# Between two layers of a transformer trunk: inverse roots, modulation and low parts change engines, and small matmuls change order

## The chip, the cores and the metric

One core of a Trainium2 chip runs the whole program. The engines are TensorE (PE in the profile, its weight loads PEld), VectorE (DVE), ScalarE (ACT), GpSimd (POOL) and SyncE (SP, which issues most DMAs). Each works through its own queue in order and waits there for semaphores of the others. The metric is device microseconds of one launch, the median of several runs.

## The reference

The trunk has two layers and a shared key/value step between them. D is 1024, the sequence 1024 tokens.

```python
h = _modulated_norm(x, norm_g[0], shift, scale)
y = _gdn_mixer(h, ...)                  # layer A: gated delta rule, 8 heads of 128
x = x + gate * y
hk = _modulated_norm(x, kv_norm_g, mkv[:, :D], mkv[:, D:])
kv = hk @ w_kv
k_sh = _rms(kv[..., :1024].reshape(B, T, 16, 64), k_gain); v_sh = kv[..., 1024:]
h = _modulated_norm(x, norm_g[1], shift, scale)
x = x + gate * _sb_mixer(h, k_sh, v_sh, ...)   # layer B: stick-breaking attention

# _modulated_norm: x * rsqrt(mean(x*x) + EPS) * gain * (1 + scale) + shift
```

Everything is in 32-bit floats. In layer A a unit lower triangular system of each chunk of 64 tokens is solved (`triangular_solve`).

## The kernel before

Tokens come in 8 tiles of 128. To keep 32-bit accuracy the kernel splits a matmul operand into a high part in the fast format `F32R` and a low part, the rest. `mm3` (L100 to L102) issues three matmuls for each product: high by high, high by low, low by high. So whoever makes an operand makes a high part (a cast) and then a low part (a subtraction that reads the cast).

Layer A runs up to about 700 us, a loop over 8 heads. In it `stage_d` (L549) inverts the triangular blocks of all 8 chunk pairs of a head: matmuls of 32x32 blocks into `py` (L560), copies `y1` on ACT, matmuls into `pu` (L567, L570), then the same with 64x64 blocks. The rows of a 32x32 matmul count two passes each, so 16 matmuls show as x32.

Behind it comes the stage that this text calls the bridge, about 711 to 787 us. `rest_of_a(t)` (L715) has two calls for each of the 8 tiles. The first call is the output projection of the last two heads: `split_o` brings `of` and makes `oh` (ACT, L226) and `ol` (DVE, L227), 12 matmuls of 512 columns fill `pj`, and L237 (DVE) adds the residual and gives `x2`. POOL issues its store (L727). ACT squares `x2` with a running sum (L729), DVE forms the inverse root (`rsqrt`, L86: a start value from integer operations and three Newton steps, 11 instructions on a 128x1 column, names `rsb_y` and `rsb_z`), and L732 scales `x2` in place. That write has to wait until the store of `x2` has landed (semaphores DMASW in the order's rows). The second call transposes the tile in two groups of four 128x128 blocks into the PSUM tile `ptx`, copies a group to `xh` (L740), stores `xh` for layer B, modulates its four blocks into `htk` (L744, a scale and a shift for each partition), casts the high part into `hkT` (L746, ACT) and subtracts for the low part (L747, POOL). `keys_values` then multiplies `hkT` with the key/value weights: `kv_half` (L775), matmuls of 256 columns; its norm of keys (`rnb`, 128x16) uses `rsqrt` too.

Only PE's order is written out by hand there:

```python
with tc.manual_schedule(engines={PE.engine}):
    ra, kv = [rest_of_a(t) for t in range(NT)], keys_values()
    for step in "01203w142k53k64k75kk6k7k":
        next(kv if step in "wk" else ra[int(step)], None)
```

A digit is a call for that tile (its first occurrence the projection, its second the transposes), `w` brings the first weights, `k` is one quarter of a `kv_half`, 24 matmuls. So tile 4 is projected after the transposes of tile 1, and so on. The order of the other engines' queues is made by the scheduler. `xh`, `htk` and two temporaries of `kv_half` share five buffers (tag `x2k`); `pj` has two PSUM buffers.

Of the kernel before, what the change touches and what calls it, by code (L numbers as in the profile page):

```python
# [8 lines left out]
F32 = mybir.dt.float32  # L9
F32R = mybir.dt.float32r  # L10
I32 = mybir.dt.int32
AF = mybir.ActivationFunctionType
ALU = mybir.AluOpType
# [9 lines left out]
def kernel(  # L23
# [24 lines left out]
    V, S, G, PE = nc.vector, nc.scalar, nc.gpsimd, nc.tensor  # L48
    dma = nc.sync.dma_start

    P = 128
# [5 lines left out]
    NC = T // P  # L57
# [28 lines left out]
    def rsqrt(pool, v, n, tag):  # L86

        y = pool.tile([P, n], F32, name=f"{tag}_y", tag=f"{tag}_y")
        z = pool.tile([P, n], F32, name=f"{tag}_z", tag=f"{tag}_z")
        yi = y.bitcast(I32)  # L90
        V.tensor_scalar(out=yi, in0=v.bitcast(I32), scalar1=1, scalar2=None, op0=ALU.arith_shift_right)
        V.tensor_scalar(out=yi, in0=yi, scalar1=-1, scalar2=0x5F3759DF, op0=ALU.mult, op1=ALU.add)
        for _ in range(3):
            V.tensor_tensor(out=z, in0=y, in1=y, op=ALU.mult)
            V.scalar_tensor_tensor(out=z, in0=z, scalar=-0.5, in1=v, op0=ALU.mult, op1=ALU.mult)
            V.scalar_tensor_tensor(out=y, in0=z, scalar=1.5, in1=y, op0=ALU.add, op1=ALU.mult)  # L96
        return y

    def mm3(ps, lh, ll, rh, rl, start, stop):
# [22 lines left out]
    mod_sh = [const.tile([P, ND], F32, name=f"sh{i}") for i in range(3)]  # L122
    mod_gs = [const.tile([P, ND], F32, name=f"gs{i}") for i in range(3)]
# [128 lines left out]
    with tc.tile_pool(name="st", bufs=2, side="right", reuse_waits="tile") as st:  # L252
# [54 lines left out]
        for n0 in (0, 512):  # L307
            scale = mod_acc(st, 0, 1, n0, 512, 16)
# [7 lines left out]
            for hf in range(TH):  # L316
# [13 lines left out]
                  start=True, stop=True)  # L330
# [11 lines left out]
    with tc.tile_pool(name="gt", bufs=1, side="right", reuse_waits="tile") as gt:  # L342
# [6 lines left out]
        for cc in range(NC):  # L349
# [6 lines left out]
        y = gt.tile([P, HA, NC], F32, name="gy")  # L356
        V.tensor_tensor(out=y, in0=pbv[:, 8:16, :], in1=alb[:, 1, :][:, :, None].broadcast_to([P, HA, NC]),
                        op=ALU.add)
# [11 lines left out]
        for cf in coef[2:]:  # L370
# [10 lines left out]
                               op0=ALU.mult, op1=ALU.mult)  # L381
# [4 lines left out]
        f = lambda a: a.rearrange("p h c -> p (h c)")  # L386
# [32 lines left out]
    for i in range(2):  # L419
        U = gp.tile([P, NC, P], F32, name=f"U{i}")  # L420
# [128 lines left out]
    def stage_d(h, st):  # L549
        U, nm = st["U"], st["nm"]  # L550

        for b in range(3):
            bs = slice(32 * b, 32 * b + 32)
            c0 = 32 * (b % 2)
            V.transpose(out=tb[bs, :, c0:c0 + 32], in_=U[bs, :, bs])
        blk = [slice(32 * b, 32 * b + 32) for b in range(4)]
        py = dd_pool.tile([P, NC, 32], F32, name="py", tag="dd")
        for a in (0, 2):
            for cc in range(NC):
                PE.matmul(py[blk[a + 1], cc], nm[blk[a], cc, blk[a + 1]], tb[blk[a], cc, 0:32],  # L560
                          start=True, stop=True)
        y1 = gp.tile([P, NC, 32], F32, name="y1", tag="y1")
        for a in (0, 2):
            S.copy(out=y1[blk[a + 1]], in_=py[blk[a + 1]])
        pu = dd_pool.tile([P, NC, 32], F32, name="pu", tag="dd")
        for cc in range(NC):
            PE.matmul(pu[blk[1], cc], U[blk[1], cc, blk[1]], y1[blk[1], cc], start=True, stop=True)  # L567
        for a in (0, 2):
            for cc in range(NC):
                PE.matmul(pu[blk[a], cc], y1[blk[a + 1], cc], U[blk[a + 1], cc, blk[a + 1]],  # L570
                          start=True, stop=True)
        S.mul(out=tb[blk[1], :, 0:32], in_=pu[blk[1]], mul=-1.0)
        for a in (0, 2):
            S.mul(out=U[blk[a], :, blk[a + 1]], in_=pu[blk[a]], mul=-1.0)
        lo_, up_ = slice(0, 64), slice(64, 128)
        py = dd_pool.tile([P, NC, 64], F32, name="py2", tag="dd")
        for cc in range(NC):
            PE.matmul(py[up_, cc], nm[lo_, cc, up_], tb[lo_, cc], start=True, stop=True)
        y2 = gp.tile([P, NC, 64], F32, name="y2", tag="y2")
        S.copy(out=y2[up_], in_=py[up_])  # L580
        pu = dd_pool.tile([P, NC, 64], F32, name="pu2", tag="dd")
        for cc in range(NC):
            PE.matmul(pu[lo_, cc], y2[up_, cc], U[up_, cc, up_], start=True, stop=True)
        S.mul(out=U[lo_, :, up_], in_=pu[lo_], mul=-1.0)
# [62 lines left out]
    for h in range(HA):  # L647
# [23 lines left out]
        if h < len(mods):  # L671
            i, part = mods[h]
# [33 lines left out]
    hkT = xsp.tile([P, 2, ND, T], F32R, name="hkT")  # L706

    kp_ = kv_stack.enter_context(tc.tile_pool(name="kvp", bufs=2, side="right", reuse_waits="tile"))
# [6 lines left out]
    def rest_of_a(t):  # L715
        x2 = None
        if t in early:
            xr, o, x2 = early[t]
        else:
            o = split_o(kp_, oTa, t, rest, "of", 2, kp_, ("oh", "ol"))  # L720
            xr = x4([P, D], F32, "xr")
            dma(out=xr, in_=xs1[t])
        x2 = x2 or x4([P, D], F32, "x2")
        for hf in range(2):
            sl = slice(hf * 512, hf * 512 + 512)
            out_proj(o, wo, rest, hf, xr[:, sl], x2[:, sl])
        G.dma_start(out=xs2[t], in_=x2)  # L727
        sv = kp_.tile([P, 1], F32, name="sv", tag="sv")
        S.activation(out=xr, in_=x2, func=AF.Square, accum_out=sv)  # L729
        V.tensor_scalar(out=sv, in0=sv, scalar1=1.0 / D, scalar2=EPS, op0=ALU.mult, op1=ALU.add)  # L730
        rs = rsqrt(kp_, sv, 1, "rsb")
        V.tensor_scalar(out=x2, in0=x2, scalar1=rs, scalar2=None, op0=ALU.mult)  # L732
        yield
        ts_ = slice(t * P, (t + 1) * P)
        for kk in range(0, ND, 4):
            pt = wk_pool.tile([P, 4, P], F32, name="ptx", tag="wk")
            for i in range(4):
                PE.transpose(pt[:, i], x2[:, (kk + i) * P:(kk + i + 1) * P], ident)
            xh = kp_.tile([P, 4, P], F32, name="xh", tag="x2k", bufs=5)
            S.copy(out=xh, in_=pt)  # L740
            dma(out=xhT[kk:kk + 4, :, ts_].rearrange("k p t -> p k t"), in_=xh)
            ht = kp_.tile([P, 4, P], F32, name="htk", tag="x2k", bufs=5)
            for i in range(4):
                V.tensor_scalar(out=ht[:, i], in0=xh[:, i], scalar1=mod_gs[2][:, kk + i:kk + i + 1],  # L744
                                scalar2=mod_sh[2][:, kk + i:kk + i + 1], op0=ALU.mult, op1=ALU.add)
            S.copy(out=hkT[:, 0, kk:kk + 4, ts_], in_=ht)  # L746
            G.tensor_tensor(out=hkT[:, 1, kk:kk + 4, ts_], in0=ht, in1=hkT[:, 0, kk:kk + 4, ts_],  # L747
                            op=ALU.subtract)


# [24 lines left out]
    def kv_half(n, parts, hf):  # L775
        c0 = n * 256
        kv = x4([P, 4, 256], F32, "kv")
        n2 = kp_.tile([P, 4, 4], F32, name="n2b", tag="n2b") if n < 4 else None
# [20 lines left out]
            return  # L799
        n2 = n2.rearrange("p t g -> p (t g)")  # L800
        V.tensor_scalar(out=n2, in0=n2, scalar1=1.0 / HD, scalar2=EPS, op0=ALU.mult, op1=ALU.add)
        rn = rsqrt(kp_, n2, 16, "rnb")
        kg = kv.rearrange("p t (g d) -> p (t g) d", d=HD)
        V.tensor_tensor(out=kg, in0=kg, in1=rn[:, :, None].broadcast_to([P, 16, HD]), op=ALU.mult)
        V.tensor_tensor(out=kg, in0=kg, in1=gain[:, 2:3, :].broadcast_to([P, 16, HD]), op=ALU.mult)
# [111 lines left out]
    n2, sqs, vraw = {}, {}, {}  # L917
# [258 lines left out]
```

## Time and profile before

| what | before |
|---|---|
| median of 3 runs | 1514.25 us (1512.17 to 1517.61) |
| the profiled execution | 1510.67 us, span 1508.8 us |
| granted TensorE clock, whole span | 0.983 |
| busy in the span: PE / DVE / ACT / POOL | 1408.9 / 1074.4 / 728.0 / 151.3 us |
| bridge, 711 to 787 us: PE / DVE / ACT / POOL | 56.77 / 71.89 / 40.43 / 26.52 us of 76.00 |

A row of a table by windows has, in this order, the stretch and its length, then the busy time of PE, PEld, DVE, ACT and POOL with their counts of instructions, the granted TensorE clock as a share of full speed, the busy share of the DMA engines and what they moved. A row of the timeline has the start, the duration, engine, line and operation, the tile written and the tiles read, and in brackets the idle time ahead of it and what ended it.

### The profile page before, as it was taken

The numbers are of one execution on the slowest core, as the hardware profiler recorded it, in microseconds if no ns is written. First come the engines' busy times: TensorE is split into PE (matmuls) and PEld (weight loads), VectorE is DVE, ScalarE is ACT, GpSimd is POOL, SyncE is SP. The second block draws the span as 40 slices with busy tenths as digits, with TensorE's granted clock in tenths as the row PEclk, the third lists the DMA queues.
The fourth block names the chain that finished last, engine by engine and source line by source line (L and its number), as shares of the span: only waits on it lengthen the run. The fifth ranks groups of instructions, "written<-read, shape, count | busy, mean of one in ns | idle before, by whom it ended". The sixth has DMA issues, their size and how long they took to land.

```text
span 1508.8 us, 23724 instructions
## 1 busy us (share of the span) xinstructions
PE 1408.9 (93%) x8739; PEld 1179.8 (78%) x8739; DVE 1074.4 (71%) x2595; ACT 728.0 (48%) x1429; POOL 151.3 (10%) x121
## 2 busy tenths in 40 slices
PE   3789999999979999999689999999999999998998
PEld 1478888787868887887589999888888888885676
DVE  3768796977868697855997710478888888889332
ACT  5456645545545554422554422366566666665210
POOL 1300000000000000000330111412121121100000
PEclk9999999999989999999899999999999999999999
DMA  9144324444443444445744343624224223324511
GB/s 331 50 126 137 74 49 117 115 137 114 122 106 116 104 147 119 146 124 171 264 154 155 140 141 105 182 57 112 78 64 112 82 83 88 95 74 132 170 54 57
DMA packets 175303, 181.18 MB, mean 120 GB/s; under 512 B 36617, under 2 KB 129618, under 8 KB 175186
## 3 DMA queue, kind: packets, MB, share of 16 engines
q1 hardware_dynamic: 174034, 175.46, 39.1%
q0 software_dynamic: 1152, 4.19, 0.7%
q8 instruction: 69, 1.13, 0.3%
q14 instruction: 48, 0.39, 0.1%
HBM read 140.22 MB, written 39.40 MB: 119 GB/s over the span
## 4 chain that ended last, share of the span: by engine, by line
PE 61%; DVE 26%; ACT 5%; DMA 4%; issue 2%; SPq 1%; POOL 0%; DVEq 0%; ACTq 0%
PE pj L100 14%; PE pj L102 14%; PE pj L101 14%; DVE kp L977 7%; DMA mraw<-in_w_ada_dram 2%; DVE wl L998 2%; PE ptw L991 2%; PE pgr L473 2%; DVE macc L139 2%; PE pa L1016 1%; ACT whi L183 1%; PE pa L1017 1%; DVE htk L744 1%; PE pl L968 1%; DVE qk L412 1%
## 5 line engine op out<-in xcount | busy, mean ns | idle before, releaser
L100 PE MATMUL pj<-hT,whi 128*128 128x512 f32 (+1 forms) x528 | 216.2, 410 | 6.0 <-ACT vT L410 3.1
L102 PE MATMUL pj<-hT,wlo 128*128 128x512 f32 (+1 forms) x528 | 215.8, 410 | 4.5 <-DVE wlo L184 4.4
L101 PE MATMUL pj<-hT,whi 128*128 128x512 f32 (+1 forms) x528 | 215.1, 407 | 1.2 <-POOL hT L298 1.2
L977 DVE TENSOR_TENSOR_SCAN kp<-kp 128x896 f32<-128x896 f32 (+7 forms) x128 | 190.4, 1490 | 12.1 <-ACT kp L973 10.8
L973 ACT ACTIVATE kp<-pl,nrq 128x512 f32<-128x512 f32 (+1 forms) x192 | 107.1, 580 | 54.8 <-PE pl L972 39.0
L996 ACT ACTIVATE wh<-ptw 128x512 fp32r<-128x512 f32 (+3 forms) x152 | 84.6, 557 | 71.8 <-PE ptw L991 70.1
L100 PEld LDWEIGHTS pj<-hT,whi 128*128 128x128 f32 (+1 forms) x528 | 99.1, 188 | 25.4 <-ACT vT L410 3.8
L102 PEld LDWEIGHTS pj<-hT,wlo 128*128 128x128 f32 (+1 forms) x528 | 98.9, 187 | 23.5 <-DVE wlo L184 5.8
L101 PEld LDWEIGHTS pj<-hT,whi 128*128 128x128 f32 (+1 forms) x528 | 98.9, 187 | 19.9 <-POOL hT L298 2.3
L100 PE MATMUL pj<-hbT,whi 128*128 128x512 f32 x256 | 110.0, 430 | 0.0
L100 PE MATMUL pj<-wo,oh 128*128 128x512 f32 x256 | 104.2, 408 | 5.9 <-DVE rsb_y L96 2.5
L102 PE MATMUL pj<-wo,ol 128*128 128x512 f32 x256 | 102.6, 401 | 7.1 <-DVE ol L227 7.1
L101 PE MATMUL pj<-wo,oh 128*128 128x512 f32 x256 | 102.7, 401 | 0.0
L102 PE MATMUL pj<-hbT,wlo 128*128 128x512 f32 x256 | 101.6, 397 | 0.0
L101 PE MATMUL pj<-hbT,whi 128*128 128x512 f32 x256 | 101.0, 394 | 0.0
L998 DVE SCALAR_TENSOR_TENSOR wl<-ptw,wh 128x512 fp32r<-128x512 f32 (+1 forms) x140 | 87.1, 623 | 11.8 <-ACT wh L996 10.8
L991 PE MATMUL ptw<-ident,kp 128*128 128x128 f32 x576 | 91.1, 276 | 3.9 <-DVE wl L998 3.0
L1016 PE MATMUL pa<-wh,vt 128*128 128x256 f32 (+1 forms) x280 | 79.7, 307 | 14.0 <-DVE o L1027 13.3
L183 ACT CAST whi<-wraw 128x1024 fp32r<-128x1024 f32 x55 | 57.7, 1049 | 67.4 <-PE pj L101 55.5
L139 DVE SCALAR_TENSOR_TENSOR macc<-mraw,cact,macc 128x512 f32<-128x512 f32 x105 | 82.2, 783 | 6.3 <-DMA mraw<-in_w_ada_dram 5.3
L991 PEld LDWEIGHTS ptw<-ident,kp 128*128 128x128 f32 x576 | 68.1, 141 | 22.3 <-DVE wl L998 9.3
L100 PE MATMUL pj<-whi,hkT 128*128 128x256 f32 x256 | 73.7, 288 | 4.6 <-DVE x L237 3.9
(302 smaller groups left out, 3498.4 us busy)
## 6 DMA issues: line engine op xcount, KB each, us to landing
mraw<-in_w_ada_dram SPq DMA_DIRECT2D x96, 256.0 KB
wraw<-in_w_in_a_dram SPq DMA_DIRECT2D x32, 512.0 KB
mraw<-in_w_ada_kv_dram SPq DMA_DIRECT2D x32, 256.0 KB
xr<-x_dram SPq DMA_DIRECT2D x16, 512.0 KB
wraw<-in_w_kv_dram SPq DMA_DIRECT2D x16, 512.0 KB
kT_dram<-kt SPq DMA_DIRECT2D x32, 256.0 KB
wraw<-in_w_in_b_dram SPq DMA_DIRECT2D x16, 512.0 KB
Kh<-kT_dram SPq DMA_DIRECT2D x32, 256.0 KB
```

Of the source, the lines that this page charges most:

```text
L100: PE.matmul(ps, lh, rh, start=start, stop=False)
L101: PE.matmul(ps, lh, rl, start=False, stop=False)
L102: PE.matmul(ps, ll, rh, start=False, stop=stop)
L139: V.scalar_tensor_tensor(out=acc, in0=raw, scalar=cact[:, k:k + 1], in1=acc, op0=ALU.mult, op1=ALU.add)
L183: (copy or S.copy)(out=hi, in_=raw)
L473: PE.matmul(pg[:, ii], qk[:, 1, sl], qk[:, :, sl], start=True, stop=True)
L973: S.activation(out=kp[:, s0:s0 + sw], in_=pl[:, :sw], func=AF.Sigmoid, scale=nrq[p][:, t, e:e + 1])
L977: V.tensor_tensor_scan(out=kr, data0=kr, data1=kr, initial=1.0, op0=ALU.mult, op1=ALU.bypass)
L991: PE.transpose(pt[:, i], kps[p, e, 2 * g + q][:, j * P:(j + 1) * P], ident)
L996: S.activation(out=wh[:, :nb], in_=pt[:, :nb], func=AF.Copy, bias=-1.0)
L998: V.scalar_tensor_tensor(out=wl[:, :nb], in0=pt[:, :nb], scalar=-1.0, in1=wh[:, :nb], op0=ALU.add, op1=ALU.subtract)
L1016: PE.matmul(dst, lh, wh[:, sl], start=(j == 0), stop=False)
```

## The change

Four edits. First, the two inverse roots behind layer A (`rsb`, `rnb`) come from a new `rsqrt_act`: ACT's square root, DVE's reciprocal and one Newton step, so 1 instruction on ACT and 4 on DVE in place of 11. Second, the copy of `ptx` to `xh` goes from ACT to DVE, and the modulation from DVE (reading `xh`) to ACT (reading `ptx`). Third, the low part of `hkT` goes from POOL to DVE. Fourth, in `stage_d` the small matmuls of two independent block columns alternate.

```diff
+    def rsqrt_act(pool, v, n, tag):
...
+        S.activation(out=z, in_=v, func=AF.Sqrt)
+        V.reciprocal(out=y, in_=z)
+        V.tensor_tensor(out=z, in0=y, in1=y, op=ALU.mult)
+        V.scalar_tensor_tensor(out=z, in0=z, scalar=-0.5, in1=v, op0=ALU.mult, op1=ALU.mult)
+        V.scalar_tensor_tensor(out=y, in0=z, scalar=1.5, in1=y, op0=ALU.add, op1=ALU.mult)
         return y
...
-        for a in (0, 2):
-            for cc in range(NC):
+        for cc in range(NC):
+            for a in (0, 2):
                 PE.matmul(py[blk[a + 1], cc], nm[blk[a], cc, blk[a + 1]], tb[blk[a], cc, 0:32],
...
         for cc in range(NC):
             PE.matmul(pu[blk[1], cc], U[blk[1], cc, blk[1]], y1[blk[1], cc], start=True, stop=True)
-        for a in (0, 2):
-            for cc in range(NC):
-                PE.matmul(pu[blk[a], cc], y1[blk[a + 1], cc], U[blk[a + 1], cc, blk[a + 1]],
-                          start=True, stop=True)
+            PE.matmul(pu[blk[2], cc], y1[blk[3], cc], U[blk[3], cc, blk[3]], start=True, stop=True)
+        for cc in range(NC):
+            PE.matmul(pu[blk[0], cc], y1[blk[1], cc], U[blk[1], cc, blk[1]], start=True, stop=True)
...
-        rs = rsqrt(kp_, sv, 1, "rsb")
+        rs = rsqrt_act(kp_, sv, 1, "rsb")
...
-            S.copy(out=xh, in_=pt)
+            V.tensor_copy(out=xh, in_=pt)
...
-                V.tensor_scalar(out=ht[:, i], in0=xh[:, i], scalar1=mod_gs[2][:, kk + i:kk + i + 1],
-                                scalar2=mod_sh[2][:, kk + i:kk + i + 1], op0=ALU.mult, op1=ALU.add)
+                S.activation(out=ht[:, i], in_=pt[:, i], func=AF.Identity, scale=mod_gs[2][:, kk + i:kk + i + 1],
+                             bias=mod_sh[2][:, kk + i:kk + i + 1])
             S.copy(out=hkT[:, 0, kk:kk + 4, ts_], in_=ht)
-            G.tensor_tensor(out=hkT[:, 1, kk:kk + 4, ts_], in0=ht, in1=hkT[:, 0, kk:kk + 4, ts_],
+            V.tensor_tensor(out=hkT[:, 1, kk:kk + 4, ts_], in0=ht, in1=hkT[:, 0, kk:kk + 4, ts_],
...
-        rn = rsqrt(kp_, n2, 16, "rnb")
+        rn = rsqrt_act(kp_, n2, 16, "rnb")
```

PE's order is the same but for the small matmuls. The queues of ACT and DVE come out of the scheduler in another order. Lines of the changed kernel count 11 more than those of before up to the small matmuls (10 more behind them).

On ACT, at the start of the bridge, stood these rows before; `x_7366` is the `x2` of tile 2, `x_7439` that of tile 3, and the cast of `oh` of tile 4 is the one directly behind the square of `x_7366`.

```order
L729 ACTIVATE xr,sv<-x_7323 128x1024 [waits DMAHW2_49,DVE_49]
L226 CAST oh<-of 128x256 [waits DMAHW6_49]
L226 CAST oh<-of 128x256 [waits DMAHW1_49]
L740 COPY xh<-ptx 128x512 [waits PE_49] x2
L729 ACTIVATE xr,sv<-x_7366 128x1024 [waits DMAHW0_49,DVE_49]
L226 CAST oh<-of 128x256 [waits DMAHW3_49,Activation_49]
L746 CAST hkT<-htk 128x4x128 [waits DMAHW5_49,DMAHW7_49,DMAHW4_49,DVE_49]
L770 CAST kwh<-wraw 128x1024 [waits DMAHW2_49]
L746 CAST hkT<-htk 128x4x128 [waits DVE_49]
L740 COPY xh<-ptx 128x512 [waits PE_49]
L729 ACTIVATE xr,sv<-x_7439 128x1024 [waits DMAHW4_49,DVE_49]
```

In the changed kernel the square of tile 3 is the one of `x_7421`, and the rows there are these.

```order
L780 CAST kwh<-wraw 128x1024 [waits DMAHW2_49]
L756 CAST hkT<-htk 128x4x128 [waits Activation_49]
L739 ACTIVATE xr,sv<-x_7421 128x1024 [waits DMAHW4_49,DVE_49]
L754 ACTIVATE htk<-ptx,sh_95,gs_98 128x128 [waits DVE_49]
L754 ACTIVATE htk<-ptx,sh_95,gs_98 128x128 x2
L103 ACTIVATE rsb_z<-sv 128x1 [waits DVE_49]
L754 ACTIVATE htk<-ptx,sh_95,gs_98 128x128
L237 CAST oh<-of 128x256 [waits DMAHW3_49]
L756 CAST hkT<-htk 128x4x128 [waits Activation_49]
```

The cast of `oh` that stood behind the square of tile 2 now stands behind the square of tile 3, four modulations and a square root; the first modulation of each group waits for DVE, which copies the same PSUM tile.

On DVE, around the in-place scaling of tile 2 (the row that waits for DMASW2, the landed store), stood these rows before.

```order
L744 TENSOR_SCALAR htk<-xh,gs_98,sh_95 128x128 [waits DMAHW6_49,Activation_49]
L732 TENSOR_SCALAR x_7366<-x_7366,rsb_y 128x1024 [waits DMASW2_49,DVE_49]
L94 TENSOR_TENSOR rsb_z<-rsb_y 128x1 [waits DVE_49]
L744 TENSOR_SCALAR htk<-xh,gs_98,sh_95 128x128
L95 SCALAR_TENSOR_TENSOR rsb_z<-rsb_z,sv 128x1 [waits DVE_49]
L744 TENSOR_SCALAR htk<-xh,gs_98,sh_95 128x128
L96 SCALAR_TENSOR_TENSOR rsb_y<-rsb_z,rsb_y 128x1 [waits DVE_49]
L744 TENSOR_SCALAR htk<-xh,gs_98,sh_95 128x128
L94 TENSOR_TENSOR rsb_z<-rsb_y 128x1 [waits DVE_49]
L227 TENSOR_TENSOR ol<-of,oh 128x256 [waits DMAHW3_49]
```

In the changed kernel these stand there (`x_7354` is tile 2, `x_7421` tile 3).

```order
L757 TENSOR_TENSOR hkT<-htk,hkT 128x4x128 [waits DMAHW3_49,Activation_49]
L742 TENSOR_SCALAR x_7354<-x_7354,rsb_y 128x1024 [waits DMASW2_49,DVE_49]
L248 TENSOR_TENSOR x_7421<-pj,xr 128x512 [waits PE_49]
L750 COPY xh<-ptx 128x512 [waits PE_49]
L757 TENSOR_TENSOR hkT<-htk,hkT 128x4x128 [waits Activation_49]
L781 TENSOR_TENSOR kwl<-wraw,kwh 128x1024 [waits DMAHW2_49]
L740 TENSOR_SCALAR sv<-sv 128x1 [waits Activation_49]
L750 COPY xh<-ptx 128x512 [waits DMAHW6_49,PE_49]
```

The scaling of tile 2 has moved ahead of the second add of tile 3, which stood before it; the four modulations and the Newton operations between them are gone, two copies of `xh` and two low parts have come in.

On PE, in the first head, the small matmuls of `pu` were one run for each block column before.

```order
L100 MATMUL pj<-hT,whi 128x512
L567 MATMUL pu<-y_1451,U_633 32x32 x8
L570 MATMUL pu<-U_633,y_1451 32x32 x16
L101 MATMUL pj<-hT,whi 128x512
L102 MATMUL pj<-hT,wlo 128x512
```

In the changed kernel they alternate; the pair of rows stands eight times.

```order
L111 MATMUL pj<-hT,whi 128x512
L578 MATMUL pu<-y_1451,U_633 32x32
L579 MATMUL pu<-U_633,y_1451 32x32
...
L581 MATMUL pu<-U_633,y_1451 32x32 x8
L112 MATMUL pj<-hT,whi 128x512
```

The eight matmuls of L567 and the second eight of L570 now take turns, and the first eight of L570, which stood between them, come last. `py` is treated alike: its two runs of eight take turns.

## Rows read from the trace of the kernel before

**Rows 1.** Windows: length, busy PE, PEld, DVE, ACT, POOL, PEclk, DMA share, GB/s

```profile
711.00:787.00 76.00, 56.77 (x347) 49.88 (x346) 71.89 (x218) 40.43 (x77) 26.52 (x24) 0.89 0.64 212
732.20:787.00 54.80, 47.35 (x300) 43.08 (x301) 52.05 (x145) 28.24 (x55) 20.46 (x17) 0.89 0.53 172
726.80:736.90 10.10, 4.63 (x11) 3.60 (x12) 9.86 (x31) 2.83 (x5) 4.41 (x3) 0.50 0.72 236
747.20:750.60 3.40, 3.40 (x18) 3.40 (x17) 3.29 (x12) 1.92 (x4) 1.77 (x2) 0.50 0.72 248
764.30:767.60 3.30, 3.30 (x17) 3.30 (x17) 3.30 (x15) 1.63 (x5) 1.09 (x2) 0.50 0.80 249
787.00:870.00 83.00, 83.00 (x706) 83.00 (x705) 61.13 (x151) 37.12 (x76) 10.50 (x8) 1.00 0.43 151
```

**Rows 2.** Waits of PE, 711 to 787: us in total, times, longest

```profile
PE pj L100 <- DVE x L237: 3.9, 2, 2.0
PE pj L102 <- POOL hkT L747: 2.7, 4, 0.8
PE pj L100 <- DVE rsb_y L96: 2.5, 1, 2.5
```

**Rows 3.** Timeline of PE at the bridge's longest wait: start us, us, what

```profile
732.27 0.80 PE L102 MATMUL pj<-wo,ol 128*128 128x512 f32 x1 [7.08 <-DVE ol L227]
```

**Rows 4.** Timeline of DVE: start us, us, line, operation, shapes

```profile
726.13 1.23 DVE L95 SCALAR_TENSOR_TENSOR rsb_z<-rsb_z,sv 128x1 f32<-128x1 f32 x1
727.28 0.33 DVE L744 TENSOR_SCALAR htk<-xh,gs,sh 128x128 f32<-128x128 f32 x1
727.54 0.15 DVE L96 SCALAR_TENSOR_TENSOR rsb_y<-rsb_z,rsb_y 128x1 f32<-128x1 f32 x1
...
729.02 0.73 DVE L732 TENSOR_SCALAR x<-x,rsb_y 128x1024 f32<-128x1024 f32 x1
```

**Rows 5.** Timeline of POOL at the same place and just before

```profile
719.14 0.53 POOL L727 DMA_DIRECT2D x_dram<-x  x1 [5.60 <-DVE rsb_z L95]
...
725.89 1.45 POOL L747 TENSOR_TENSOR hkT<-htk,hkT 128x512 fp32r<-128x512 f32 x1
```

**Rows 6.** The tile htk, 711 to 787: ns min/median/max, first, last start

```profile
L744 DVE TENSOR_SCALAR htk<-xh,gs,sh x64: 326/340/1391, 718.8 to 781.6; 128x128 f32<-128x128 f32 x64
...
L747 POOL TENSOR_TENSOR hkT<-htk,hkT x16: 1262/1291/2427, 722.1 to 783.7; 128x512 fp32r<-128x512 f32 x16
```

**Rows 7.** Chain that ended last, 711 to 740: start us, us, what

```profile
713.00 6.95 DMA x_dram<-x
...
723.74 0.60 DVE x L237
```

**Rows 8.** ACT by line, 711 to 787: busy us, mean ns, idle before

```profile
L740 ACT COPY xh<-ptx 128x512 f32<-128x512 f32 x16 | 9.0, 579 | 3.8 <-PE ptx L738 3.3 <-POOL hkT L747 0.5
L729 ACT ACTIVATE xr<-x 128x1024 f32<-128x1024 f32 x8 | 8.5, 1059 | 15.4 <-DVE x L237 15.4
...
L226 ACT CAST oh<-of 128x256 fp32r<-128x256 f32 x6 | 2.4, 403 | 7.9 <-PE pj L101 4.2 <-DMA of<-oTa_dram 3.7
```

**Rows 9.** Groups of ACT by line and shape, whole kernel

```profile
L446 ACT ACTIVATE kdec<-ptk,gA 128x128 f32<-128x128 f32 x64 | 18.3, 389 | 2.2 <-PE pS L610 2.2
...
L295 ACT ACTIVATE ht<-pt,sh,gs 128x512 f32<-128x512 f32 x16 | 12.0, 775 | 18.8 <-PE pt L293 14.0 <-POOL hT L298 2.7 <-DVE hT L298 1.0
...
L955 ACT ACT_TABLE_LOAD x1 | 1.3, 1283 | 0.0
```

**Rows 10.** Timeline of PE around the small matmuls of one head

```profile
361.50 1.09 PE L560 MATMUL py<-tb,nm 32*32 32x32 f32 x32
...
363.65 0.59 PE L567 MATMUL pu<-y,U 32*32 32x32 f32 x13
364.06 0.21 PE L570 MATMUL pu<-U,y 32*32 32x32 f32 x1
...
365.08 0.50 PE L100 MATMUL pj<-hT,whi 128*128 128x512 f32 x1
```

More of the change, by code (lines that the diff above doesn't have):

```diff
@@ L96, in rsqrt @@
             V.scalar_tensor_tensor(out=y, in0=z, scalar=1.5, in1=y, op0=ALU.add, op1=ALU.mult)
+        return y
+    def rsqrt_act(pool, v, n, tag):
+        y = pool.tile([P, n], F32, name=f"{tag}_y", tag=f"{tag}_y")
+        z = pool.tile([P, n], F32, name=f"{tag}_z", tag=f"{tag}_z")
+        S.activation(out=z, in_=v, func=AF.Sqrt)
[3 more added lines that the diff above has]
+        V.scalar_tensor_tensor(out=y, in0=z, scalar=1.5, in1=y, op0=ALU.add, op1=ALU.mult)
         return y
```

## The prediction

> **What bounds the kernel now.** I read the windows first. Behind the bridge, from 787 us on, PE is busy without a gap (83.00 of 83.00 us at full clock), so nothing that the change frees on DVE, ACT or POOL there can shorten it; the `rnb` half of the first edit is worth nothing for that reason, with PE's work as its cover. The bridge is different: of its 76.0 us PE works 56.77, DVE 71.89, ACT 40.43 [rows 1]. DVE is the full engine, PE has 19.2 us of idle time, and three stretches (10.1, 3.4 and 3.3 us) run at a granted clock of 0.50, the 1.2 GHz level, with 4.63, 3.40 and 3.30 us of PE work in them. At 2.4 GHz that work takes half, so the low level costs 11.33/2 = 5.7 us. PE's floor in the bridge is 56.8 - 5.7 = 51.1 us, and the most that could be gained there is 76.0 - 51.1 = 24.9 us.
>
> The waits say what PE is idle for: the adds of the projection on DVE 3.9, POOL's low parts 2.7, the inverse root's last step 2.5 [rows 2], and one wait of 7.08 us for `ol` on DVE [rows 3]. The rest of the 19.2, 3.0, is ACT's casts. The long wait ends at 732.27. Ahead of 732.2 PE worked 56.77 - 47.35 = 9.4 of 21.2 us; behind it 47.35 of 54.8 [rows 1]. So I treat the bridge as a start and a rest. The rest loses 7.45 us to idle time (the adds 3.9, the low parts 2.7, a cast 0.8) and (3.40 + 3.30)/2 = 3.35 us to the clock; the start loses 11.8 and 2.3.
>
> Why is DVE full? The timeline of DVE shows a Newton operation on one column that takes 1.23 us (726.13 to 727.36) where its neighbour of the same kind takes 0.15 [rows 4]. POOL's low part ran from 725.89 to 727.34 [rows 5]: DVE's operation stood until POOL's ended. A modulation takes 340 ns in the median and 1391 at worst, and POOL's low part 1291 [rows 6]; 16 of those, each costing DVE about 1391 - 340 = 1.05 us, are an estimated 16 us of DVE's 71.9.
>
> **The change, by engine.** DVE loses 64 modulations at 0.26 from start to next start (727.28 to 727.54) [rows 4], 16.6 us, the 16 us of holding, and 7 of 11 root operations in 8 tiles, 56 at between nothing (slotted into a neighbour's time) and 0.15 [rows 4]: 0 to 8.4 us, and I take 5, as a small operation in a chain of its own is rare there. It gains 16 copies and 16 low parts. No 512-column copy from PSUM on DVE is in the bridge; the add of that width from PSUM takes 0.60 in the chain [rows 7], so 32 x 0.60 = 19.2. After: 71.9 - 16.6 - 16 - 5 + 19.2 = 53.5 us.
>
> ACT loses 9.0 us of copies [rows 8]. A modulation of 128x128 from PSUM with a scale and a shift column isn't in the trace. Below it lies the 128x128 with one column operand: 389 ns each, and 18.3/64 = 0.286 us of busy time apiece since they overlap. The two column operands of a 512-wide one bring it to 775 [rows 9], against 579 of the plain copy [rows 8]: 98 ns each. So 0.286 + 0.098 = 0.384 is the value I take, 24.6 us for 64, with 18.3 and (no overlap) 31 as the ends. To this come 8 square roots at about 0.2 (between DVE's 0.15 and ACT's 0.389 for 128 columns) and one table load of 1.28 [rows 9]. After: 40.4 - 9.0 + 24.6 + 1.6 + 1.3 = 58.9 (52.6 to 66). ACT becomes the fullest of the three, ahead of DVE 53.5 and PE 51.1. POOL's 16 operations go, 20.7 us, and with them the holding.
>
> The Trainium skill, ScalarE: Activation LUTs, section Rules for kernel authors, speaks against this edit: multiplication and addition belong on VectorE, not on ScalarE. The rows agree on the price, 0.26 against 0.384, that is 64 x 0.12 = 7.9 us more engine time. By that rule, all of it on the path, the gain worked out below would fall to 0.3 us; the first rival below says what makes it so here.
>
> **The start.** The store of tile 2 is issued at 719.14 [rows 5]; that of tile 1 took 6.95 us to land [rows 7]. The scaling of tile 2 waits for the landing, and in the changed order DVE's second add of tile 3 stands behind that scaling; behind it on ACT come the square of tile 3, four modulations, and only then the cast of `oh` of tile 4. Without the Newton operations in DVE's way I put the landing at 725.5, 0.6 before 719.14 + 6.95. Then scaling 0.73 [rows 4], add 0.60, square 1.06, modulations 4 x 0.384, cast 0.40 [rows 8], `ol` as long as the cast, 0.4, so 730.2 against 732.27: a gain of **2.0** (0 if the store lands 2 us later, 4 if the cast doesn't wait for the square). The low clock of the start stays, since PE still waits over 5 us.
>
> **The rest.** DVE falls from 52.05 of 54.8 us to about 39.5 (less 11 us of holding, 48 x 0.26 modulations and 3.5 of roots, plus 24 x 0.60), ACT rises from 28.24 to about 41 (less 6.7 of copies, plus 48 x 0.384 and 1 of roots), PE needs 47.35 - 3.35 = 44.0. With DVE no longer full, half of the adds' 3.9 goes (1.9). The low parts take 0.6 on DVE instead of 1.29 on POOL, but the modulation ahead of them takes 1.5 instead of 1.04 us for a group and starts behind DVE's copy; of their 3.5 I let 2.0 go. One of the two short stretches of low clock goes with the idle time ahead of it, 1.7. Sum **5.6** of the 10.8 us that the rest loses. Ends: 0, if ACT's waits take the place of DVE's, and 10.8.
>
> **The small matmuls.** `py` takes 1.09 us for 32 passes, from 361.50. In `pu` 16 passes of L567 go first, and the first L570 starts 364.06 - 363.65 = 0.41 us later, 25 ns for each pass sent ahead of it; the whole `pu` takes 365.08 - 363.65 = 1.43 for 48, 30 ns each [rows 10]. One stream alone so costs about 29 to 31 ns a pass and PE can send one each 25. Alternating brings `py` from 29 to 25: 32 x 0.0037 = 0.12 us a head, about 1 us in 8 heads. `pu` saves nothing: its third stream still starts behind 32 others. The two copies of `y1` now both wait for the end of `py`, where the first could go early: I take half of it back. **0.6** (0 to 1.7).
>
> **Sum.** 2.0 + 5.6 + 0.6 = 8.2 us. The profiled execution took 1510.67 us (span 1508.8), so 1502.5 like for like. The median shown is 1514.25, 3.6 above; against it 1506.0, which I forecast.
>
> **Rivals.** *ACT takes it back.* ACT's queue is in order, and each group goes PE, DVE, ACT, ACT, DVE. A square or an `oh` cast that stands behind a modulation waits for DVE's copy too. For it: ACT at 41 of some 49 us in the rest is nearly as full as DVE was; the first modulation of each group waits on DVE. Against: DVE's own holding is gone. Gain 0 to 4.5, about 1512.
>
> *Full relief.* Without holding, all waits of the rest fall away and the clock stays up: 10.8, with a start that ends another 2 us earlier: 2.0 + 2 + 10.8 + 0.6 = 15.4, up to 22 if the start closes further; 1492 to 1499. For it: 16 us of holding are more than all that PE waits. Against: ACT at 58.9 us allows a bridge of no less, and it isn't busy in the first microseconds.
>
> *The streams run side by side.* If two alternating streams overlap wholly, `py` saves half of 1.09 - 0.21 (one pass, which the pair still needs) and `pu` one stream of 0.41 [rows 10]: 0.85 us a head, 6.8 us in 8, instead of 0.6. Against: PE's sends are 25 ns apart in [rows 10] though the blocks of L567 and L570 differ. It gives 1500. The Trainium skill, TensorEngine Tiling (Array Packing), section Key Properties, states this rule, that different tiles can execute in parallel; no row here shows two passes sent together.
>
> *Slower: the cast of `oh` is late each time.* The start's pattern, `oh` behind modulations behind a copy, repeats for tiles 5, 6 and 7. If each lost what the start loses now at `ol`, 7.1 us of idle time and 2.3 of clock, three times 9.4 = 28 would stand where 10.8 are lost now: 17 more, less 2.6 from start and small matmuls, so +14, 1528. It decides when a tile loses more than (10.8 + 2.6)/3 = 4.5 us. Against: from tile 5 on `k` steps of 24 matmuls lie between, 24 x 83.00/706 = 2.8 us of PE work each [rows 1], which cover part of such a delay.
>
> **Chances and range.** Forecast 0.58 (1500 to 1509.5, gain 4.5 to 14), full relief 0.12, streams side by side 0.05, ACT takes it back 0.17, slower 0.08. About 0.3%, 4.5 us, is what a measurement of this kernel can tell from no change. Faster is forecast, relief and streams: 0.75; the same 0.17; slower 0.08. The range leaves out the slower case and the far end of relief: 1494 to 1513.5.
>
> **What would show it.** Right: in the changed profile no DVE operation on one column above 0.3 us in the bridge; DVE near 53 and ACT near 59 us there; the modulation near 0.48 us long; the long wait near 732 ending some 2 us earlier and now on ACT's cast; `py` near 1.0 us. Wrong: low-clock stretches that grow, waits of PE on `oh` at tiles 5 to 7, a modulation above 0.5 us apiece from start to start, or DVE still held where no POOL work is left.

## The result, and the profile after

The changed kernel takes 1495.11 us (median of 6 runs, 1493.37 to 1504.48), the kernel before 1513.99 on the same occasion (6 runs). The ratio is 0.9884, with a 95% interval of 0.9857 to 0.9911: by the ratio 17.6 us less, by the two medians 18.9, where 8.2 were forecast. The profiled execution has a span of 1491.7 us, 17.1 less than before's 1508.8.

Where the 17.1 us came from is read by three landmarks in the timeline of PE: the first wait of the bridge, the first matmul of the next stage (on `hbT`), and the end. The bracket of a row is the idle time ahead of it and what ended it. Before:

```profile
714.27 0.50 PE L100 MATMUL pj<-wo,oh 128*128 128x512 f32 x1 [2.30 <-ACT oh L226]
...
952.02 0.40 PE L100 MATMUL pj<-hbT,whi 128*128 128x512 f32 x1
```

The changed kernel:

```profile
704.24 0.50 PE L111 MATMUL pj<-wo,oh 128*128 128x512 f32 x1 [2.31 <-ACT oh L237]
...
719.93 0.80 PE L111 MATMUL pj<-wo,oh 128*128 128x512 f32 x1 [5.99 <-ACT oh L237]
...
720.95 0.63 PE L113 MATMUL pj<-wo,ol 128*128 128x512 f32 x1
...
936.42 0.40 PE L111 MATMUL pj<-hbT,whi 128*128 128x512 f32 x1
```

The first wait of the bridge ends at 704.24, 10.03 us earlier than before. The next stage begins 15.60 us earlier, and the end comes 17.1 earlier. So layer A gave 10.0 us of the 17.1, the bridge 5.6, and what lies behind it 1.6; there before's trace has a stretch of 3.4 us at a granted clock of 0.50 (from 975.9) and the other, at that place, has 1.00. The 10.0 us are of two single executions: in the traces of before and of the five runs below that leave layer A as it was, the first wait of the bridge ends anywhere from 714.27 to 719.45. The long wait is now for `oh` on ACT and ends at 719.93; the third matmul of tile 4's projection, the one that started at 732.27 in [rows 3], starts at 720.95, which is 730.98 on before's scale.

The window of the changed kernel that ends at the same place in PE's work as before's (787, less the 15.6), with the columns of [rows 1].

```profile
701.00:771.40 70.40, 53.71 (x348) 46.36 (x347) 53.71 (x121) 54.20 (x135) 3.89 (x8) 0.95 0.68 225
```

DVE fell from 71.89 of 76 us to 53.71 of 70.4 (53.5 forecast), ACT rose from 40.43 to 54.20 (58.9 forecast), and the granted clock from 0.89 to 0.95. All three engines are about equally full. The waits of PE in the bridge, in us in all, times, longest:

```profile
PE pj L111 <- ACT oh L237: 8.3, 2, 6.0
PE pj L111 <- DVE x L248: 2.7, 2, 1.6
PE pj L111 <- ACT kv L796: 2.3, 2, 1.3
PE ptx L748 <- ACT htk L754: 1.8, 2, 1.0
PE pj L111 <- ACT hkT L756: 0.8, 1, 0.8
```

The adds fell from 3.9 to 2.7, the low parts no longer stand there with more than 0.4, and ACT, by `oh`, `kv`, `htk` and `hkT`, ends 13.2 us of PE's idle time. The tiles `htk` and `rsb_z` (ns min/median/max, first and last start):

```profile
L754 ACT ACTIVATE htk<-ptx,sh,gs x64: 439/458/487, 709.3 to 767.3; 128x128 f32<-128x128 f32 x64
```

```profile
L103 ACT ACTIVATE rsb_z<-sv x8: 197/202/217, 702.4 to 753.0; 128x1 f32<-128x1 f32 x8
L104 DVE RECIPROCAL rsb_y<-rsb_z x8: 151/160/164, 702.7 to 753.2; 128x1 f32<-128x1 f32 x8
...
L106 DVE SCALAR_TENSOR_TENSOR rsb_z<-rsb_z,sv x8: 150/159/160, 703.1 to 753.6; 128x1 f32<-128x1 f32 x8
```

No one-column operation of DVE in the bridge is above 164 ns: the holding of [rows 4] is gone. The small matmuls of one head, timeline of PE, to be held against [rows 10]:

```profile
358.30 0.69 PE L571 MATMUL py<-tb,nm 32*32 32x32 f32 x32
358.92 0.50 PE L113 MATMUL pj<-hT,wlo 128*128 128x512 f32 x1
...
360.05 0.21 PE L578 MATMUL pu<-y,U 32*32 32x32 f32 x1
360.06 0.21 PE L579 MATMUL pu<-U,y 32*32 32x32 f32 x1
...
361.08 0.50 PE L111 MATMUL pj<-hT,whi 128*128 128x512 f32 x1
```

`py` takes 358.92 - 358.30 = 0.62 us to the next matmul, where before the next one came 1.02 us later; `pu` takes 361.08 - 360.05 = 1.03, where it took 1.43. Each saves 0.40 us in a head where no other matmul comes between. The forecast had 0.1 and nothing.

### The profile page after: what moved, and what is told of

It reads as the page before. It is cut to its first block, busy times and chain, and to the rows that moved or that the text cites. A ratio compares the mean times of both kernels' runs of the same rounds, so it can differ in the third digit from the quotient of the medians.

```text
span 1491.7 us, 23618 instructions
## 1 busy us (share of the span) xinstructions
PE 1395.3 (94%) x8739; PEld 1166.1 (78%) x8739; DVE 1049.5 (70%) x2451; ACT 744.3 (50%) x1494; POOL 128.6 (9%) x105
## 4 chain that ended last, share of the span: by engine, by line
PE 61%; DVE 25%; ACT 7%; DMA 4%; issue 2%; SPq 0%; DVEq 0%; ACTq 0%
PE pj L111 15%; PE pj L112 14%; PE pj L113 14%; DVE kp L987 8%; DVE wl L1008 2%; PE ptw L1001 2%; PE pgr L484 2%; DMA mraw<-in_w_ada_dram 2%; DVE macc L150 2%; PE pa L1026 1%; ACT whi L194 1%; PE pa L1027 1%; PE pl L978 1%; PE pl L980 1%; ACT kp L983 1%
## 5 line engine op out<-in xcount | busy, mean ns | idle before, releaser
L1006 ACT ACTIVATE wh<-ptw 128x512 fp32r<-128x512 f32 (+3 forms) x152 | 84.7, 557 | 70.4 <-PE ptw L1001 68.5
L1008 DVE SCALAR_TENSOR_TENSOR wl<-ptw,wh 128x512 fp32r<-128x512 f32 (+1 forms) x140 | 87.3, 624 | 11.4 <-ACT wh L1006 10.4
```

Source lines behind the costliest of these rows:

```text
L1006: S.activation(out=wh[:, :nb], in_=pt[:, :nb], func=AF.Copy, bias=-1.0)
L1008: V.scalar_tensor_tensor(out=wl[:, :nb], in0=pt[:, :nb], scalar=-1.0, in1=wh[:, :nb], op0=ALU.add, op1=ALU.subtract)
```

## The experiments

Times are medians, with the kernel before measured on the same chip. A ratio is the one on record with its 95% interval; it isn't exactly that of the two medians. A gain in us is worked out from the ratio.

**The small matmuls alone.** The kernel before with the fourth edit and nothing else.

```diff
-        for a in (0, 2):
-            for cc in range(NC):
+        for cc in range(NC):
+            for a in (0, 2):
                 PE.matmul(py[blk[a + 1], cc], ...)
...
             PE.matmul(pu[blk[1], cc], U[blk[1], cc, blk[1]], y1[blk[1], cc], start=True, stop=True)
+            PE.matmul(pu[blk[2], cc], y1[blk[3], cc], U[blk[3], cc, blk[3]], start=True, stop=True)
```

> The kernel before with the fourth edit alone, the small matmuls taking turns. Theory A (streams of different block rows run side by side): py from 0.90 to 0.50 us and pu from 1.31 to 0.91 us from first to last start, in all 8 heads but one or two whose run is interrupted, so 6.4 us off the heads, and the time falls by 6 to 10 us, to about 1505. Theory B (the 10 us that layer A lost in the trace came mostly from stretches of low clock that differ between executions): the small matmuls shorten as in A, but the time falls by no more than 6.5 us. Theory C (the forecast, a send every 25 ns): the time falls by 0 to 1.7 us.

1505.95 us against 1515.59, ratio 0.9938 (0.9916 to 0.996): 9.4 us. `py` and `pu` shorten as theory A said, and the price that the forecast put on them is refuted. In the trace of this kernel the eight `py` and eight `pu`, from first to last start, are 5.4 us shorter in all (the last head's `pu` is interrupted by other matmuls and grows by 0.3). That is less than 9.4, though near the interval's lower end of 6.1; the run with `py` twice, below, is about the difference.

**The bridge alone.** The changed kernel with the small matmuls in the old order.

```diff
-        for cc in range(NC):
-            for a in (0, 2):
+        for a in (0, 2):
+            for cc in range(NC):
                 PE.matmul(py[blk[a + 1], cc], ...)
```

(`pu` goes back to the old order as well.)

> The changed kernel with the small matmuls in the old order: the edits of the bridge alone. If the terms of the bridge in the forecast hold (2.0 for the start, 5.6 for the rest), the time falls by 7 to 8 us against the kernel before, to about 1506, and layer A ends as late as in the kernel before (its first projection of the bridge within 1 us). If the bridge gave more than that and the heads less, the time is below 1502.

1508.12 us against 1515.59, ratio 0.995 (0.993 to 0.997): 7.6 us, the 2.0 + 5.6 of the forecast. Layer A, which this kernel leaves as it was, should have ended within 1 us of before's: its trace has the first wait of the bridge end at 716.82, 2.55 us later, so the 7.6 aren't from there. The two halves add up: 9.4 + 7.6 = 17.0, against 17.6 for the whole.

**Which streams run side by side.** In `pu`, L578 and L579 now read the same block row and write different block columns.

```diff
             PE.matmul(pu[blk[1], cc], U[blk[1], cc, blk[1]], y1[blk[1], cc], start=True, stop=True)
-            PE.matmul(pu[blk[2], cc], y1[blk[3], cc], U[blk[3], cc, blk[3]], start=True, stop=True)
+            PE.matmul(pu[blk[0], cc], y1[blk[1], cc], U[blk[1], cc, blk[1]], start=True, stop=True)
         for cc in range(NC):
-            PE.matmul(pu[blk[0], cc], y1[blk[1], cc], U[blk[1], cc, blk[1]], start=True, stop=True)
+            PE.matmul(pu[blk[2], cc], y1[blk[3], cc], U[blk[3], cc, blk[3]], start=True, stop=True)
```

> The changed kernel with another pairing in pu: L578 (block row 1 into block column 1) takes turns with the product of block row 1 into block column 0, and block row 3 comes last. If streams run side by side only when their block rows (the partitions read) differ, pu takes 1.25 to 1.35 us again, while py stays at 0.50. If different block columns (the partitions written) are enough, pu takes 0.9. If what matters is only that neighbours in the queue are different, 0.9 as well.

1499.25 us in one run. The timeline of PE in the same head:

```profile
363.97 0.21 PE L578 MATMUL pu<-y,U 32*32 32x32 f32 x1
363.97 0.21 PE L579 MATMUL pu<-U,y 32*32 32x32 f32 x1
...
365.00 0.50 PE L111 MATMUL pj<-hT,whi 128*128 128x512 f32 x1
```

The pairs start together, and `pu` takes 365.00 - 363.97 = 1.03 us, as in the changed kernel. So it isn't the block row: different block columns are enough. Streams that share the block column and differ in the block row alone were not run.

**All three in turn.**

```diff
             PE.matmul(pu[blk[2], cc], y1[blk[3], cc], U[blk[3], cc, blk[3]], start=True, stop=True)
-        for cc in range(NC):
             PE.matmul(pu[blk[0], cc], y1[blk[1], cc], U[blk[1], cc, blk[1]], start=True, stop=True)
```

> The changed kernel with all three products of pu taking turns. If a stream of one block row has a pass each 25 ns and another block row runs beside it, the 32 passes of block row 1 set the time: about 0.81 us to the last start, 0.1 less than the 0.91 of the changed kernel. If the third product makes the queue wait in order, 0.9 or more. The time is within 2 us of the changed kernel's either way.

1498.53 us in one run. The timeline of PE:

```profile
362.61 0.21 PE L578 MATMUL pu<-y,U 32*32 32x32 f32 x1
362.62 0.21 PE L579 MATMUL pu<-U,y 32*32 32x32 f32 x1
362.62 0.21 PE L580 MATMUL pu<-U,y 32*32 32x32 f32 x1
362.66 0.19 PE L578 MATMUL pu<-y,U 32*32 32x32 f32 x1
...
363.24 0.50 PE L111 MATMUL pj<-hT,whi 128*128 128x512 f32 x1
```

Three passes start within 0.01 us, the second of the first stream 0.05 later, and `pu` takes 363.24 - 362.61 = 0.63 us. I expected 0.1 us less than the changed kernel and got 0.40 less. The 48 passes take 0.51 us from first to last start, the 16 of L567 alone took 0.50 before (363.65 to 364.15): a pass waits only for the one ahead of it in its own block, some 30 ns. (The time of a single run says nothing here: layer A and the parts behind had other stretches of low clock.)

**Each edit of the bridge alone.** First the low parts on DVE.

```diff
-            G.tensor_tensor(out=hkT[:, 1, kk:kk + 4, ts_], in0=ht, ...)
+            V.tensor_tensor(out=hkT[:, 1, kk:kk + 4, ts_], in0=ht, ...)
```

> The kernel before with the third edit alone: the low parts of hkT on DVE, not on POOL. Theory H (POOL's low parts held DVE for some 16 us, and that made most of the waits): no one-column operation of DVE in the bridge above 0.3 us, DVE's busy time in the bridge falls by about 5 us although it has 16 operations of 0.69 more, and the time falls by 3 to 6 us. Theory M (the holding cost PE little; the move of the modulation did the work): the same picture on DVE, but the time falls by less than 2 us.

1511.02 us against 1513.32, ratio 0.9976 (0.9959 to 0.9993): 3.6 us. The holding is gone (a modulation takes at most 347 ns, where [rows 6] had 1391) and DVE works 65.87 of 76 us, from 711 to 787, where it worked 71.89. The 16 low parts, 683 ns each, add 10.9 us there, so some 17 us went, near the 16 estimated for the holding. The tile `htk`, and PE's waits between 711 and 800 us:

```profile
L744 DVE TENSOR_SCALAR htk<-xh,gs,sh x64: 334/341/347, 721.4 to 776.7; 128x128 f32<-128x128 f32 x64
```

```profile
PE pj L102 <- DVE ol L227: 8.2, 1, 8.2
PE pk L809 <- DVE kv L805: 5.2, 1, 5.2
```

The long wait for `ol` stays, and a new one of 5.2 us comes in, for the key norm on DVE.

Then the modulation on ACT and the copy to `xh` on DVE.

```diff
-            S.copy(out=xh, in_=pt)
+            V.tensor_copy(out=xh, in_=pt)
...
-                V.tensor_scalar(out=ht[:, i], in0=xh[:, i], ...)
+                S.activation(out=ht[:, i], in_=pt[:, i], func=AF.Identity, ...)
```

> The kernel before with the second edit alone: the copy to xh on DVE, the modulation on ACT, low parts still on POOL. Theory H: POOL's 16 operations go on holding DVE, now the copies and adds, so the time falls by no more than 2 us. Theory M: DVE loses 64 operations and gains 16, about 6 us less, and the time falls by 3 to 6 us.

1519.03 us against 1513.32, ratio 1.0031 (1.0013 to 1.0049): 4.7 us slower. Neither theory had that. PE's waits:

```profile
PE pj L100 <- ACT oh L226: 9.3, 2, 7.0
PE ptx L738 <- ACT htk L744: 3.4, 3, 1.3
```

`oh` ends 9.3 us of idle time, its longest wait 7.0, where it ended 2.3 before. This is the late cast of the rival that I had as slower, at one place only.

Then both together, without the new roots (the two diffs above).

> The kernel before with the second and the third edit, without the new roots and with the small matmuls in the old order. Alone they gave -3.6 and +4.7 us. If they only add, the time is 1 us above the kernel before. If the move of the modulation pays only when POOL no longer holds DVE, the time falls by 4 to 7 us, and the new roots are worth the rest of the 7.6 us of all three.

1509.04 us against 1513.00, ratio 0.9965 (0.9949 to 0.998): 5.3 us. They don't add (-3.6 and +4.7 would be 1 us slower): the move of the modulation costs time with the low parts on POOL, and costs nothing that shows with them on DVE.

Then the new roots alone.

```diff
-        rs = rsqrt(kp_, sv, 1, "rsb")
+        rs = rsqrt_act(kp_, sv, 1, "rsb")
...
-        rn = rsqrt(kp_, n2, 16, "rnb")
+        rn = rsqrt_act(kp_, n2, 16, "rnb")
```

> The kernel before with the first edit alone: the inverse roots from ACT's square root and one Newton step. Theory R (DVE's queue was so full that 56 operations less count): DVE's busy time in the bridge falls by 4 to 6 us and the time by 2 to 5. Theory H (held by POOL, DVE stays full and the roots slip between): POOL's holding moves to other operations, the long wait for ol stays near 7 us, and the time falls by no more than 2 us.

1507.26 us against 1513.00, ratio 0.9949 (0.9931 to 0.9967): 7.7 us, as much as all three edits of the bridge together. POOL still holds DVE here; the groups of DVE by line (busy us, mean ns, idle time before) and the waits of PE:

```profile
L755 DVE TENSOR_SCALAR htk<-xh,gs,sh 128x128 f32<-128x128 f32 x64 | 23.7, 418 | 1.4 <-ACT xh L751 0.9 <-ACT rsb_z L103 0.4
...
L106 DVE SCALAR_TENSOR_TENSOR rsb_z<-rsb_z,sv 128x1 f32<-128x1 f32 x8 | 4.5, 559 | 0.1
```

```profile
PE pj L113 <- DVE ol L238: 4.3, 1, 4.3
PE pj L111 <- DVE x L248: 3.3, 3, 1.5
...
PE pj L113 <- POOL hkT L758: 2.2, 4, 0.8
```

A one-column step takes 559 ns in the mean, so the holding is there, and still the wait for `ol` is 4.3 us, not 7.1. The trace says the same as the time: from the first wait of the bridge to the first matmul on `hbT` it takes 718.71 to 950.00, 231.3 us, where before took 237.8. DVE works 66.81 of the 76 us that correspond to before's 711 to 787 (715.44 to 791.44), 5.1 less. Theory R holds, its time above the 2 to 5 us that it gave.

**The low parts back on POOL.** The changed kernel with one line as before.

```diff
-            V.tensor_tensor(out=hkT[:, 1, kk:kk + 4, ts_], in0=ht, ...)
+            G.tensor_tensor(out=hkT[:, 1, kk:kk + 4, ts_], in0=ht, ...)
```

> The changed kernel with the low parts of hkT on POOL again. Theory H: DVE operations of over 1 us on small tiles come back, PE waits on POOL's low parts again, and the time is 3 to 7 us above the changed kernel's, about 1500. Theory M: within 2 us of the changed kernel.

1501.69 us against 1513.32, ratio 0.9918 (0.9891 to 0.9944), where the changed kernel has 0.9884: some 5 us worse, as theory H says, though the two intervals overlap. PE waits for POOL's low parts again (1.4 us in 3 waits), and a one-column step takes up to 691 ns.

**`py` twice.** The kernel before, each product of `py` computed twice (the second writes the same values).

```diff
-        for a in (0, 2):
+        for a in (0, 2, 0, 2):
             for cc in range(NC):
                 PE.matmul(py[blk[a + 1], cc], ...)
```

> The kernel before with each product of py computed twice, one stream behind the other in the old order: 0.90 us more in each of 8 heads, 7.2 us of PE work. Theory D (a small matmul costs what its row shows): the time rises by 6 to 8 us. Theory F (the heads pay more than the row, since the granted clock falls more often behind a stretch of small matmuls or the work that waits for them comes late): the time rises by 10 us or more and the mean granted clock falls below 0.979. The other way round, that is why the fourth edit gave 9.4 us where its rows show 5 to 6.4.

1527.69 us against 1513.00, ratio 1.0079 (1.0052 to 1.0106): 12.0 us (7.9 to 16.0). The added work is somewhat less than the 7.2 us that I had expected: `py` of this head takes 376.40 - 374.56 = 1.84 us to the next matmul, 0.82 more than the 1.02 of before, so an estimated 6.6 us in 8 heads. The mean granted clock of its four runs is 0.975 to 0.979, that of the kernel before 0.976 to 0.985 (median 0.981 of 15). The timeline of PE, and windows of this kernel:

```profile
374.56 1.91 PE L560 MATMUL py<-tb,nm 32*32 32x32 f32 x64
376.40 0.50 PE L100 MATMUL pj<-hT,whi 128*128 128x512 f32 x1
376.74 2.38 PE L163 MATMUL pc<-ones,macc 128*128 128x1 f32 x16
```

```profile
377.90:384.70 6.80, 6.80 (x25) 5.69 (x24) 1.35 (x4) 2.08 (x7) 0.00 (x0) 0.50 0.59 155
456.40:463.20 6.80, 6.80 (x42) 5.27 (x40) 0.00 (x0) 4.58 (x13) 0.00 (x0) 0.50 0.63 169
370.00:377.90 7.90, 7.60 (x95) 6.31 (x94) 4.86 (x14) 4.77 (x8) 0.00 (x0) 1.00 0.12 20
```

A stretch of 6.8 us at 0.50, the 1.2 GHz level, begins at 377.9, directly behind a stretch with PE busy 7.60 of 7.90 us, in which 64 of the 95 rows are passes of `py`; another of 6.8 us begins at 456.4. But it isn't `py` alone that stands ahead of the first: it begins while the 16 one-column matmuls of L163 run. The interval does reach down to 7.9 us, so theory F isn't beyond doubt by the time alone; the mean clock speaks for it.

**Two further edits on the changed kernel.** All three of `pu` in turn, and the scaling of `x2` into the buffer of `xr`.

```diff
-        V.tensor_scalar(out=x2, in0=x2, scalar1=rs, scalar2=None, op0=ALU.mult)
+        V.tensor_scalar(out=xr, in0=x2, scalar1=rs, scalar2=None, op0=ALU.mult)
+        x2 = xr
         yield
```

> The changed kernel with two further edits: all three products of pu take turns, and the scaled x2 goes into the buffer of xr (which holds only the squares by then), so that it needs not wait for the store of x2 to land. From the first, 0.4 us in each of 7 heads, 2.8 us. From the second, the wait of DVE for that store (5.3 us in 7 waits in the changed kernel) goes, and the cast of oh of tile 4 stands ahead of the square of tile 2 again: of PE's longest wait, 6.0 us, I expect 3 to 5 back. About 1488 (1484 to 1492). Rival: the xr buffers, kept longer, are late for the next tile's loads, and only the 2.8 us stay: 1492.

1492.26 us against 1513.32, ratio 0.9854 (0.9827 to 0.9881): 22.1 us below the kernel before, 4.5 more than the changed kernel's 17.6 by the two ratios; their intervals overlap. I had expected 1488, and 1492 if only the 2.8 us of `pu` came; yet the start did come back, as the timeline of PE shows:

```profile
715.07 0.66 PE L748 MATMUL ptx<-ident,xr 128*128 128x128 f32 x4 [1.26 <-ACT htk L754]
715.49 0.48 PE L111 MATMUL pj<-wo,oh 128*128 128x512 f32 x1
...
721.27 1.11 PE L748 MATMUL ptx<-ident,xr 128*128 128x128 f32 x4 [2.80 <-ACT htk L754]
```

The long wait for `oh` is gone: the projection of tile 4 starts at 715.49, where it started at 719.93, though the bridge begins 0.8 us later than in the changed kernel (705.00). Part of it goes again to PE's transposes, which wait for the modulations that hold the PSUM tile `ptx`, up to 2.80 us. From the first wait to the first matmul on `hbT` this bridge takes 228.5 us (705.00 to 933.47), the changed kernel's 232.2. So the two traces differ by 3.7 us in the bridge, as expected of the second edit; the 2.8 us of `pu` don't show in the start of the bridge, and the second edit was not run alone.

**The modulations off PSUM.** On top of that, they read `xh`.

```diff
-                S.activation(out=ht[:, i], in_=pt[:, i], func=AF.Identity, ...)
+                S.activation(out=ht[:, i], in_=xh[:, i], func=AF.Identity, ...)
```

> The kernel with all of the changed kernel, all three products of pu in turn and the scaled x2 in the buffer of xr, and besides the modulations read xh, not ptx, so that ptx is free for PE's next transposes after DVE's copy. The waits of PE's transposes for the modulations (6.5 us in 5 waits without this edit) go; the cast of oh of tile 5 now stands behind three more groups of modulations on ACT. If the transposes' wait was on the path: 1488 to 1491. If the late cast takes it back: 1492 to 1498.

1497.63 us against 1513.00, ratio 0.9884 (0.9862 to 0.9907): no better than the changed kernel, at the end of the range for a late cast. The waits of the transposes went, and others took their place:

```profile
PE pj L111 <- DVE x L248: 7.4, 3, 4.7
PE pk L819 <- DVE kv L815: 3.3, 1, 3.3
```

## Why the prediction was right, and where it was not

**Direction and range** held, the range by luck: 1495.11 lies 1.1 us inside its lower end, which was set for *Full relief*, and full relief did not come; PE still waits over 16 us in the bridge. The gain is more than twice the one forecast. The bridge's sum held (7.6 forecast, 7.6 measured alone); the small matmuls were mis-sized, and with them the sum.

**The small matmuls (0.6 forecast, 9.4 measured alone).** The step that failed is "PE can send one each 25": I took it that 16 passes of L567 go ahead of the first L570, and read the 0.41 us between the two in [rows 10] as the pace at which PE sends. Only 13 had gone, as the x13 of that row says: 0.41/13 is 32 ns, the pace of one stream alone, and the last three L567 run beside the first L570. The trace of before had the answer in the rows that the group leaves out, where the two lines meet:

```profile
364.08 0.19 PE L567 MATMUL pu<-y,U 32*32 32x32 f32 x1
364.11 0.19 PE L570 MATMUL pu<-U,y 32*32 32x32 f32 x1
364.11 0.19 PE L567 MATMUL pu<-y,U 32*32 32x32 f32 x1
```

L570 and L567 start within 0.01 us of each other there. The rival of streams side by side (chance 0.05) was the right one: 0.40 us each for `py` and `pu` in an undisturbed head, near its 0.85 for both, and with three streams three abreast. The sign that I named, `py` near 1.0 us, failed with 0.62. By the Trainium skill, TensorEngine Tiling (Array Packing), section Key Properties, different tiles execute in parallel; the traces agree, with starts 0.01 us apart.

**The clock behind the small matmuls** was not in the forecast at all. The rows show 5.4 us less work, the ratio 9.4 us less time, and some 6.6 us more work became 12.0 us. The mean granted clock moves with it: a median of 0.984 with the fourth edit alone against 0.980 of the kernel before on that chip, 0.9775 with `py` twice against 0.981. An estimate from these, as if PE worked through every low stretch: 0.004 of 1515 us is 6 us, which with 5.4 makes 11.4 at most, for 9.4 measured; 0.0035 of 1513 is 5.3, which with 6.6 makes 11.9, for 12.0. That the clock is the rest of the gain is supported by these means alone; no run changed the clock alone. That it falls less often behind these matmuls is not shown: with the fourth edit alone the trace still has two stretches of 3.4 us at 0.50 that begin within a few us behind small matmuls (510.7 and 592.7), as before's has (371.7 and 597.0). Layer A has less low clock there in another place, near 419, where PE waits: 6.8 us instead of 13.7. One trace of each can't settle it.

**The start (2.0 forecast).** The walk held step by step. The scaling of tile 2, after the store has landed, starts at 715.25, which is 725.28 on before's scale (725.5 forecast), and the chain runs through the add, the square of tile 3, the modulations and the cast of `oh`, as forecast:

```profile
715.25 0.75 DVE x L742
716.01 0.61 DVE x L248
...
716.64 1.15 ACT xr L739 x2
717.79 1.05 ACT htk L754 x3
...
719.59 0.30 ACT oh L237
```

It ends 0.8 us later than I had it, since a square root and the scaled sum of tile 3 stand inside the row of modulations; the gain was 732.27 - 730.98 = 1.3.

**The rest (5.6 forecast).** The bridge gave 5.6 in the trace, so 4.3 behind the 1.3 of the start; the run with the bridge alone gave 7.6 in time, so the two measures leave the term between 4 and 6. The modulation came at 24.8/64 = 0.388 us of busy time (0.384 forecast) and 461 ns each. The granted clock of the bridge has one low stretch left instead of three.

**Right sum, other shares.** I put the rest down to DVE no longer being full, mostly by the end of POOL's holding (11 us of DVE's time) and of the modulations (12.5), and little by the roots (3.5). The experiments divide it otherwise: with the holding left in place and only the roots changed, the time falls by 7.7 us, as much as with all three edits; taking the holding away alone gave 3.6, far less than the estimated 16 us that it cost DVE. But a share depends on what else is changed. On top of the other two edits the roots are worth 7.6 - 5.3 = 2.3 us (the intervals of the two runs overlap), and the low parts some 5 (the run with them back on POOL). So the two remedies overlap, and neither is the cause by itself. What I take to be the reason is argued and not shown: the eleven one-column operations of a root, each behind a neighbour that POOL could hold, stood ahead of `ol` and the adds. The rival is the order of the queues, which the scheduler makes anew with each edit; no run kept the order and changed the roots alone. The move of the modulation to ACT costs 4.7 us alone; the rival *ACT takes it back* was right about the mechanism (`oh` behind the modulations, 9.3 us of waits instead of 2.3), and the roots and low parts outweighed it. By the Trainium skill, ScalarE: Activation LUTs, section Rules for kernel authors, multiplication and addition belong on VectorE; this case's runs agree as far as that edit alone goes, 1.0031.

Open: the new roots with the small matmuls in turn, and nothing else, were not run together. By the two runs apart, 7.7 and 9.4 us, that would equal the whole change with two edits fewer, if they add. Nor were the new roots with the low parts on DVE and the modulation left there.

## What to carry to other kernels

When small matmuls use different blocks of the array, write them so that neighbours in the queue use different blocks, and look for the place in the old trace where two streams meet: their starts there give the price. A chain of short dependent operations in a full queue can cost more than its busy time; try the chain ahead of what PE waits for by itself before moving work between engines, and measure each edit both alone and on top of the others. A stretch of small matmuls can be worth more than its rows: here 9.4 us for 5.4, with a higher mean granted clock; the way from the one to the other is open.

## What the runs showed of the hardware

- Passes of 32x32 matmuls that write different block columns started within 0.01 us of each other, also where both read the same block row; three streams took 0.63 us to the next matmul, two in turn with a third behind them 1.03, three one after another 1.43.
- Some stretches of TensorE's clock at 0.50 began where the rows show PE nearly full, among small matmuls: with `py` computed twice, two of 6.8 us, at 377.9 and 456.4, the first behind 7.90 us with PE busy 7.60.
- A DVE operation that POOL's subtraction of 128x512 met ran until that ended (1.23 us for a one-column step); with POOL's low parts gone, no one-column step in the bridge was above 0.164 us. An estimated 16 us of holding cost the kernel 3.6 us when it was taken away alone.
